# Second feed-forward output of a two-layer block: the sum for the second block product made one step earlier, four loads in another order, and a plan that starts with two engines taken

## The chip, the cores and the metric

The kernel runs on one core of a Trainium2 chip. Five engines work at the same time, each through its own instruction list in the order written: TensorE (PE in the profile, its weight loads PEld), VectorE (DVE), ScalarE (ACT), GpSimd (POOL) and SyncE (SP, which issues the loads). They wait for each other by semaphores. The metric is the device time of one execution in microseconds (us); the time before is the median of three runs.

## The reference

A block of depth 2 on 512 tokens with 1024 features: layer 0 has a gated recurrent mixer, layer 1 a dilated attention, and each is followed by a feed-forward part. All is float32. Only the feed-forward part of layer 1 matters here:

```python
D_MODEL, SEQ, D_FF = 1024, 512, 2816

def swiglu_ffn(u, w_in, w_out):
    gate, up = jnp.split(u @ w_in, 2, axis=-1)
    return (jax.nn.silu(gate) * up) @ w_out

# in reference(), for each layer, with mod = cond @ ada_w[layer] + ada_b[layer]
# split into sh1, sc1, g1, sh2, sc2, g2
        u = rms_norm(h, norm_g[layer, 2]) * (1.0 + sc2) + sh2
        y = swiglu_ffn(u, ffn_w_in[layer], ffn_w_out[layer])
        h = h + (1.0 + g2) * rms_norm(y, norm_g[layer, 3])
```

## The kernel before

**Float32 by parts.** Every operand of a matmul is split into a high part (a cast on ACT) and a low part (operand minus high part, on DVE). A product of two operands is three matmuls: high by high, high by low, low by high. So each new operand costs one ACT and one DVE instruction before TensorE can use it.

**The last step before the output.** The products into the 2816 hidden features run in `seven_products`, a loop over blocks of 128 features with seven block products in place of eight (the Strassen–Winograd form). The hidden features land in `midt`, the names of whose rows are `mid`. In the last pass of that loop an `OutStart` object is called (`sooner()`); it makes the first operands of the output stage: a high and a low part of a quarter of `mid`, the high and low parts of quarter 0 of the first weights in `uh` and `ul`, and the difference of weight quarters 1 and 0. The loop keeps short sums in `W`, a view of the tile `shared`, in eight places of 256 columns, half of them for even and half for odd passes.

**The output stage.** `out_planned` computes `mid` by the second weights: 11 blocks of 256 hidden features. The first four blocks (SEVEN = 4) are taken together as a matrix of two by two quarters and again multiplied with seven products: F, E, a second F, U, Z, a second E and a second U (the names are those of the PSUM banks that they add into; two banks each). Their four pairs of features are called a11, a12, a21, a22, the weight quarters 0 to 3. The other blocks, from block 4 on, are plain products with all four names. On TensorE the order is: F, E, block 4 into F and Z, second F, block 5 into F and Z, U, Z, block 4 into E, second E, second U, block 5 into E, blocks 4 and 5 into U, then blocks 6 to 10. Each of the seven products has four steps j = 0 to 3 of six matmuls. A step needs the cut operand of `mid` (`a_cut`: `hiq`, `loq`, a ring of two) and the cut quarter of the weights of its step (`b_cut`: `uh`, `ul`, a ring of four). A plain block needs its weights cut by halves (`plain_splits`, from `rawx`) and two rows of `mid` cut into `uh` and `ul` places.

Before the change the operand of product E is the sum a21 + a22 (`first_sum`), that of U this sum minus a11 (`second_sum`), that of the second U is a11 − a21 (`third_sum`), and the second E's is a12 minus the operand of U (`fourth_sum`). Weight quarters are overwritten with differences while the products run (`b_sub`).

**What sets the order.** `out_planned` does not issue instructions but adds tasks to a `Plan`, each with its engine, an assumed cost, what it reads and writes. The plan gives every task a due time, worked back from an ideal TensorE order, and runs a list scheduling with several rules; the trial in which TensorE ends first sets the order of every engine, SP's loads too. The plan assumes that all engines are free at its start. The instructions of the loop before (`seven_products`) are in a hand-written order. `ada` items are a conditioning vector's weights, accumulated on DVE (four instructions a load) into `shared`, then summed over partitions by an all-reduce on POOL, for the gate of the last update.

**Loads.** `items` lists all weight loads in order; the SP queue issues them in that order. Two places (`raw`) hold them throughout; the output stage opens four more (`rawx`), whose memory is that of tiles which `seven_products` reads until its last matmuls with `th`, `tl` and `spare`. Quarters 0 and 1 go to the two `raw` places. The list `turn` in `planner` says which place is used next; `done_with_raw` frees one and adds a load.

Of the kernel before, what the change touches and what calls it, by code (L numbers as in the profile page):

```python
# [11 lines left out]
F32 = mybir.dt.float32  # L12
# [305 lines left out]
def block_kernel(tc, x, c, positions, ada_w, ada_b, norm_g, hgrn_w_in, lower, hgrn_norm_g, hgrn_w_out,  # L318
# [8 lines left out]
    with ExitStack() as ctx:  # L327
# [249 lines left out]
        items += f1a + quarter_items() + f1b[SEVEN:SEVEN + 2] + last_gate[0] + f1b[SEVEN + 2:SEVEN + 3] + last_gate[1] + last_gate[2]  # L577
# [321 lines left out]
        def seven_products(fs, mid, seeded, spare, th, tl, sooner=None):  # L899
# [86 lines left out]
            with tc.manual_schedule(engines=ORDERED):  # L986
# [10 lines left out]
                for i in range(len(fs)):  # L997
# [42 lines left out]
        class OutStart:  # L1040
# [8 lines left out]
            def __call__(self):  # L1049
                self.ring = st.part_tiles(0)  # L1050
                (hi, lo), src = self.a_place(0), groups_of(self.midt, 0, 0, 0)
                act.copy(PLACED2(hi), SEEN2(src))
                dve.tensor_sub(PLACED2(lo), SEEN2(src), PLACED2(hi).bitcast(F32))
                for k in range(4):
                    raw = st.raw[st.done][:, k * 512:k * 512 + 512]
                    act.copy(uh[:, k], raw)
                    dve.tensor_sub(ul[:, k], raw, uh[:, k].bitcast(F32))
                for k in range(4):
                    one, two = (st.raw[st.done + q][:, k * 512:k * 512 + 512] for q in range(2))
                    dve.tensor_sub(one, two, one)  # L1060

        def out_planned(midt, begun, roll, parts):
# [3 lines left out]
            plan, ticks, at_item, ready_first, _, mm_of, slot, PE, ACT, DVE, POOL, COPY, done_with_raw, next_weights, split_place, products, condition = planner(extra, len(items), SEVEN)  # L1066
            raws = [next_weights() for _ in range(SEVEN)]
# [82 lines left out]
            def plain_splits(j):  # L1150
                raw, p = next_weights(), split_place(0)
# [54 lines left out]
            product(E, first_sum, 0, True, lambda j, b: b_sub(j, 0, 3, 0))  # L1206
# [8 lines left out]
            done_with_raw(2)  # L1215
# [6 lines left out]
            product(U, third_sum, 1, False)  # L1222
# [476 lines left out]
        def planner(extra=(), end=0, held=0):  # L1699
# [1053 lines left out]
```

## Time and profile before

| what | value |
|---|---|
| runs (median; lowest to highest) | 1438.81 us; 1438.64 to 1441.27 us, 3 runs |
| profiled execution | 1441.98 us, span 1440.2 us |
| TensorE busy | 1406.5 us, 98% of the span |
| VectorE, ScalarE, GpSimd busy | 1152.0 (80%), 823.0 (57%), 209.8 us (15%) |
| granted TensorE clock, mean | 0.995 |
| output stage, first matmul to the span's end | 1315.4 to 1440.2 us |

The times of the trace are microseconds from the start of the span. A row of the timeline has the start, the duration, the engine, the line, the operation with what it writes and reads, how often, and in brackets the idle time of its engine before it and what ended that. Successive instructions of one engine can overlap by a few hundredths or tenths of a microsecond, so the distance from start to start is the price in a full queue, not the duration. Row of a wait: the engine, the line, what it waited for, the time in total, how often, the longest. The line numbers are those of the code above; in the changed kernel the same lines stand up to 27 further down.

### The profile page before, as it was taken

The page shows a single profiled execution, that of the slowest core. Times are in us where ns is not written, and L with a number is a line of the kernel's source. Part 1 is how long each engine was busy: PE and PEld are TensorE (multiplying, and loading weights), DVE is VectorE, ACT ScalarE, POOL GpSimd, SP SyncE. Part 2 cuts the span into 40 slices and gives each one's busy share as a digit, 9 for nine tenths or more (in the row PEclk, how much of TensorE's full clock was granted, in tenths as well). Part 3 has the DMA queues.
Part 4 walks back from the last instruction along what each step waited for, and adds up shares of the span by engine and source line. Part 5 has one row for each costly group of instructions (what it writes and reads, how often), then busy time and mean ns, then how long its engine had stood idle before and what let it go on. Part 6 is the DMA issues. An engine that isn't in the chain of part 4 may idle for free. (4 is left out here: it accounts for less than half of the span.)

```text
span 1440.2 us, 25201 instructions
## 1 busy us (share of the span) xinstructions
PE 1406.5 (98%) x9785; PEld 1303.5 (91%) x9785; DVE 1152.0 (80%) x1836; ACT 823.0 (57%) x1538; POOL 209.8 (15%) x179
## 2 busy tenths in 40 slices
PE   8999999999999999999999999999999999999998
PEld 6788899899999988888998989999988999998887
DVE  4499889587888799687887877888776978887984
ACT  4443434465555543376647878478886555555651
POOL 1013112130111112140001010001012211110030
PEclk9999999999999999999999999999999999999999
DMA  9565655132344377423253452444351334444341
GB/s 309 163 217 191 205 176 176 59 111 77 108 117 118 118 267 270 142 104 128 66 164 111 126 137 66 122 138 136 104 204 66 117 90 118 118 118 166 127 176 59
DMA packets 213896, 201.09 MB, mean 140 GB/s; under 512 B 8920, under 2 KB 170640, under 8 KB 213520
## 3 DMA queue, kind: packets, MB, share of 16 engines
q1 hardware_dynamic: 210800, 192.71, 42.8%
q10 hardware_dynamic: 1952, 6.65, 1.2%
q8 instruction: 77, 1.26, 0.4%
q0 software_dynamic: 1024, 0.12, 0.2%
q14 instruction: 43, 0.35, 0.1%
HBM read 192.30 MB, written 5.30 MB: 137 GB/s over the span
## 5 line engine op out<-in xcount | busy, mean ns | idle before, releaser
L1836 PE MATMUL ps_mm<-apart,hiq 128*128 128x256 f32 (+1 forms) x608 | 138.3, 322 | 2.1 <-ACT xs L2328 1.2
L1836 PE MATMUL ps_mm<-uh,hiq 128*128 128x256 f32 (+1 forms) x416 | 134.8, 324 | 2.8 <-ACT ps_mm L2303 2.8
L1836 PE MATMUL ps_mm<-uh,loq 128*128 128x256 f32 (+1 forms) x416 | 131.4, 316 | 0.2 <-DVE loq L2261 0.2
L1836 PE MATMUL ps_mm<-ul,hiq 128*128 128x256 f32 (+1 forms) x416 | 131.3, 316 | 0.0
L1836 PEld LDWEIGHTS ps_mm<-apart,hiq 128*128 128x128 f32 x608 | 100.8, 193 | 8.1 <-ACT xs L2328 1.7
L966 DVE TENSOR_TENSOR loq<-raw,hiq 128x1024 fp32r<-128x1024 f32 x72 | 85.0, 1221 | 20.1 <-ACT hiq L962 20.1
L975 PE MATMUL ps_mm<-th,hiq 128*128 128x256 f32 x360 | 99.0, 275 | 0.0
L975 PE MATMUL ps_mm<-tl,hiq 128*128 128x256 f32 x360 | 99.0, 275 | 0.0
L975 PE MATMUL ps_mm<-th,loq 128*128 128x256 f32 x360 | 99.0, 275 | 0.0
L1836 PE MATMUL ps_mm<-apart,loq 128*128 128x256 f32 (+1 forms) x304 | 95.8, 315 | 0.6 <-DVE loq L2350 0.6
L946 POOL TENSOR_TENSOR raw<-raw 128x512 f32<-128x512 f32 x36 | 47.9, 1331 | 319.9 <-DVE spare L942 165.2
L1836 PEld LDWEIGHTS ps_mm<-uh,hiq 128*128 128x128 f32 x416 | 79.5, 191 | 7.5 <-ACT ps_mm L2303 3.2
L962 ACT CAST hiq<-raw 128x1024 fp32r<-128x1024 f32 x72 | 72.1, 1047 | 21.1 <-DVE raw L950 16.5
L1836 PEld LDWEIGHTS ps_mm<-uh,loq 128*128 128x128 f32 x416 | 79.7, 192 | 4.7 <-DVE loq L2261 0.4
L1836 PEld LDWEIGHTS ps_mm<-ul,hiq 128*128 128x128 f32 x416 | 79.6, 191 | 4.1 <-issue 0.5
L975 PEld LDWEIGHTS ps_mm<-tl,hiq 128*128 128x128 f32 x360 | 69.1, 192 | 0.0
L975 PEld LDWEIGHTS ps_mm<-th,hiq 128*128 128x128 f32 x360 | 69.1, 192 | 0.0
L975 PEld LDWEIGHTS ps_mm<-th,loq 128*128 128x128 f32 x360 | 69.1, 192 | 0.0
L1836 PEld LDWEIGHTS ps_mm<-apart,loq 128*128 128x128 f32 x304 | 58.5, 193 | 3.9 <-DVE loq L2350 1.0
L595 PE MATMUL ps_mm<-ul,hi 128*128 128x256 f32 (+1 forms) x176 | 55.3, 314 | 1.6 <-DVE ul L694 1.6
L594 PE MATMUL ps_mm<-uh,hi 128*128 128x256 f32 (+1 forms) x176 | 55.4, 315 | 0.0
L596 PE MATMUL ps_mm<-uh,lo 128*128 128x256 f32 (+1 forms) x176 | 55.2, 314 | 0.0
(545 smaller groups left out, 4841.0 us busy)
## 6 DMA issues: line engine op xcount, KB each, us to landing
raw<-in_ffn_w_in_dram SPq DMA_DIRECT2D x144, 256.0 KB, 3.9
raw<-in_ada_w_dram SPq DMA_DIRECT2D x30, 1024.0 KB, 5.9
raw<-in_attn_w_in_dram SPq DMA_DIRECT2D x64, 256.0 KB, 4.6
raw<-in_ffn_w_out_dram SPq DMA_DIRECT2D x13, 1024.0 KB, 6.1
raw<-in_attn_w_in_dram SPq DMA_DIRECT2D x12, 1024.0 KB, 5.2
raw<-in_hgrn_w_in_dram SPq DMA_DIRECT2D x11, 1024.0 KB, 5.3
rawx<-in_ffn_w_out_dram SPq DMA_DIRECT2D x9, 1024.0 KB, 5.0
third<-in_ada_w_dram SPq DMA_DIRECT2D x8, 1024.0 KB, 7.0
```

Source lines behind the costliest of these rows:

```text
L594: pe.matmul(ps, ah, bh, start=start, stop=False, skip_group_check=part)
L595: pe.matmul(ps, ah, bl, start=False, stop=False, skip_group_check=part)
L596: pe.matmul(ps, al, bh, start=False, stop=stop, skip_group_check=part)
L946: pool.tensor_add(r[:, 2], r[:, 2], r[:, 0])
L962: act.copy(hi, src)
L966: dve.tensor_sub(lo, src, hi.bitcast(F32))
L975: pe.matmul(LAID(ps), w[x][:, a], TAKE(us[kt][y]), start=begin and kt + m == 0, stop=kt == 3 and m == 2, skip_group_check=True)
L1836: pe.matmul(LAID(dst()), x, TAKE(y), start=begin and i == 0, stop=i == len(todo) - 1, skip_group_check=True)
```

## The change

- `OutStart` now also makes the operand of product E, by halves of two features: `sum_half` adds a21 and a22 into two free places of `W` (those of the other parity), `hi_half` and `lo_half` cut it into the ring's second place. The first half is made in `__call__`, between the other operands there; the high part of the second half and its low part in `further`, which is called after the two copies of the pass. The differences of the weight quarters move into `further` too.
- `first_sum` and `third_sum` go. `second_sum` makes a21 = a11 − a21 in place and then s1 = a22 − a21, which is the same operand of U as before; the second U takes a21 as it stands. The products and their order are the same.
- The loads of the six items behind the first layer's weights are reordered: quarters 0 and 1, block 4, quarter 2, block 5, quarter 3. `turn` starts with places 2 and 4, where blocks 4 and 5 now are.
- The plan begins with two tasks without an instruction: VectorE taken for 2.6 us and ScalarE for 1.6 us.

```diff
-        items += f1a + quarter_items() + f1b[SEVEN:SEVEN + 2] + last_gate[0] + f1b[SEVEN + 2:SEVEN + 3] + last_gate[1] + last_gate[2]
+        quarters = quarter_items()
+        items += f1a + quarters[:2] + f1b[SEVEN:SEVEN + 1] + quarters[2:3] + f1b[SEVEN + 1:SEVEN + 2] + quarters[3:] + last_gate[0] + f1b[SEVEN + 2:SEVEN + 3] + last_gate[1] + last_gate[2]
...
                     if sooner and not more:
-                        sooner()
+                        sooner(W[:, 5 - i % 2:8:2])
                     run(s.first, R, 1024, B21, False)
                     act.copy(W[:, 4 + i % 2], s.both)
                     act.copy(s.u4, s.u2)
+                    if sooner and not more:
+                        sooner.further()
                     run(s.u4, Sm, 512, t1, False)
...
-            def __call__(self):
-                self.ring = st.part_tiles(0)
+            def sum_half(self, n):
+                two = slice(2 * n, 2 * n + 2)
+                dve.tensor_add(self.spare, groups_of(self.midt, 1, 0, 0)[:, two], groups_of(self.midt, 1, 1, 0)[:, two])
+
+            def hi_half(self, n):
+                act.copy(PLACED2(self.a_place(1)[0][:, 2 * n:2 * n + 2]), SEEN2(self.spare))
+
+            def lo_half(self, n):
+                hi, lo = (t[:, 2 * n:2 * n + 2] for t in self.a_place(1))
+                dve.tensor_sub(PLACED2(lo), SEEN2(self.spare), PLACED2(hi).bitcast(F32))
+
+            def __call__(self, spare):
+                self.ring, self.spare = st.part_tiles(0), spare
                 (hi, lo), src = self.a_place(0), groups_of(self.midt, 0, 0, 0)
+                self.sum_half(0)
                 act.copy(PLACED2(hi), SEEN2(src))
                 dve.tensor_sub(PLACED2(lo), SEEN2(src), PLACED2(hi).bitcast(F32))
+                self.hi_half(0)
                 for k in range(4):
                     raw = st.raw[st.done][:, k * 512:k * 512 + 512]
                     act.copy(uh[:, k], raw)
                     dve.tensor_sub(ul[:, k], raw, uh[:, k].bitcast(F32))
+                    if k == 0:
+                        self.lo_half(0)
+                        self.sum_half(1)
+
+            def further(self):
+                self.hi_half(1)
                 for k in range(4):
                     one, two = (st.raw[st.done + q][:, k * 512:k * 512 + 512] for q in range(2))
                     dve.tensor_sub(one, two, one)
+                self.lo_half(1)
...
-            raws = [next_weights() for _ in range(SEVEN)]
+            first = [next_weights() for _ in range(SEVEN + 2)]
+            raws = [first[k] for k in (0, 1, 3, 5)]
+            plain_raw = {SEVEN: first[2], SEVEN + 1: first[4]}
+            plan.add("DVE", 2.6, None, goal=-9.0)
+            plan.add("ACT", 1.6, None, goal=-9.0)
...
-            def first_sum(g):
-                a_op(g, dve.tensor_add, s1, a21, a22)
+            def second_sum(g):
+                a_op(g, dve.tensor_sub, a21, a11, a21)
+                a_op(g, dve.tensor_sub, s1, a22, a21)
                 return a_cut(0, 0, g, *s1)
-
-            def second_sum(g):
-                a_op(g, dve.tensor_sub, s1, s1, a11)
-                return a_cut(0, 0, g, *s1)
-
-            def third_sum(g):
-                a_op(g, dve.tensor_sub, a21, a11, a21)
-                return a_cut(1, 0, g)
...
-            product(E, first_sum, 0, True, lambda j, b: b_sub(j, 0, 3, 0))
+            product(E, lambda g: a_cut(1, 0, g, ready=True), 0, True, lambda j, b: b_sub(j, 0, 3, 0))
...
-            product(U, third_sum, 1, False)
+            product(U, lambda g: a_cut(1, 0, g), 1, False)
```

What this does to the engines' lists is seen at three places. The first is VectorE at the border of the two stages. In the rows, `mid_11738` is `mid`, `raw_13603` holds quarter 0, `hiq_13764` and `loq_13765` are the ring of cut `mid` operands; `ul<-raw` are low parts of weight quarters, `ul<-mid` low parts for blocks 4 and 5. Before:

```order
L984 SCALAR_TENSOR_TENSOR mid_11738<-shared 128x512
L1053 TENSOR_TENSOR loq_13765<-mid_11738,hiq_13764 128x1024
L1057 TENSOR_TENSOR ul<-raw_13603,uh 128x512 x4
L1060 TENSOR_TENSOR raw_13603<-raw_13707,raw_13603 128x512 x4
L982 TENSOR_TENSOR shared<-shared,ps_b_11891 128x256
L983 TENSOR_TENSOR shared<-shared,ps_mm_11807 128x256
L984 SCALAR_TENSOR_TENSOR mid_11738<-shared 128x512
L1122 TENSOR_TENSOR shared<-mid_11738 128x1024
L1161 TENSOR_TENSOR ul<-mid_11738,uh 128x512 x2
L1116 TENSOR_TENSOR loq_13765<-shared,hiq_13764 128x1024
L1102 TENSOR_TENSOR ul<-raw_13603,uh 128x512 x2
```

With the change:

```order
L1054 TENSOR_TENSOR shared<-mid_11738 128x2x256
L1068 TENSOR_TENSOR loq_13765<-mid_11738,hiq_13764 128x1024
L1073 TENSOR_TENSOR ul<-raw_13603,uh 128x512
L1061 TENSOR_TENSOR loq_13765<-shared,hiq_13764 128x512
L1054 TENSOR_TENSOR shared<-mid_11738 128x2x256
L1073 TENSOR_TENSOR ul<-raw_13603,uh 128x512 x3
L1082 TENSOR_TENSOR raw_13603<-raw_13707,raw_13603 128x512 x4
L1061 TENSOR_TENSOR loq_13765<-shared,hiq_13764 128x512
L983 TENSOR_TENSOR shared<-shared,ps_b_11891 128x256
L984 TENSOR_TENSOR shared<-shared,ps_mm_11807 128x256
L1188 TENSOR_TENSOR ul<-mid_11738,uh 128x512
L1129 TENSOR_TENSOR ul<-raw_13603,uh 128x512
```

The whole sum (L1122) and the low part of the sum (L1116) have gone from the place ahead of E's first low part; as halves they stand four to ten rows further up. On ScalarE, from the same border to the cast of block 4's weights, the list was this (`hiq` from `rawx` is block 4, `uh<-raw` after the two copies are E's casts):

```order
L1016 COPY ps_mm_11857<-ps_mm_11807 128x256
L1026 COPY shared<-ps_mm_11857 128x256
L1027 ACTIVATE shared<-ps_b_11889 128x256
L1160 CAST uh<-mid_11738 128x512 x2
L979 ACTIVATE shared<-ps_mm_11857 128x256
L1115 CAST hiq_13764<-shared 128x1024
L1101 CAST uh<-raw_13603 128x512
L1160 CAST uh<-mid_11738 128x512 x2
L1101 CAST uh<-raw_13603 128x512 x2
L1154 CAST hiq_13858<-rawx_13844 128x1024
L1101 CAST uh<-raw_13603 128x512
```

With the change:

```order
L1017 COPY ps_mm_11857<-ps_mm_11807 128x256
L1057 CAST hiq_13764<-shared 128x512
L1029 COPY shared<-ps_mm_11857 128x256
L1030 ACTIVATE shared<-ps_b_11889 128x256
L1187 CAST uh<-mid_11738 128x512
L1128 CAST uh<-raw_13603 128x512
L1187 CAST uh<-mid_11738 128x512 x2
L980 ACTIVATE shared<-ps_mm_11857 128x256
L1128 CAST uh<-raw_13603 128x512
L1187 CAST uh<-mid_11738 128x512
L1128 CAST uh<-raw_13603 128x512
L1181 CAST hiq_13861<-rawx_13848 128x1024
```

E's first cast now follows one cast of `mid`; its fourth still stands behind block 4's. The third place is SyncE, the loads of this stage. Before, `rawx_13842` and `rawx_13843` are quarters 2 and 3, the next two blocks 4 and 5:

```order
L87 DMA raw_13603<-in_ffn_w_out_dram 128x4x512
L87 DMA raw_13707<-in_ffn_w_out_dram 128x4x512
L87 DMA rawx_13842<-in_ffn_w_out_dram 128x4x512
L87 DMA rawx_13843<-in_ffn_w_out_dram 128x4x512
L87 DMA rawx_13844<-in_ffn_w_out_dram 128x2x1024
L87 DMA rawx_13845<-in_ffn_w_out_dram 128x2x1024
```

With the change:

```order
L87 DMA raw_13603<-in_ffn_w_out_dram 128x4x512
L87 DMA raw_13707<-in_ffn_w_out_dram 128x4x512
L87 DMA rawx_13848<-in_ffn_w_out_dram 128x2x1024
L87 DMA rawx_13849<-in_ffn_w_out_dram 128x4x512
L87 DMA rawx_13850<-in_ffn_w_out_dram 128x2x1024
L87 DMA rawx_13851<-in_ffn_w_out_dram 128x4x512
```

Block 4 is now the first of the four loads into the new places, quarter 2 the second, block 5 the third, quarter 3 the last. Beside these places, five of F's matmuls (its second step) have moved behind 24 matmuls of the last step before, and further on the accumulations of the conditioning vector and the low parts have changed places on VectorE; one accumulation more stands ahead of the additions into U.

More of the change, by code (lines that the diff above doesn't have):

```diff
@@ L1696, in block_kernel, with planner @@
         pre.close()
[L1699 removed]
+        def planner(extra=(), end=0, turn=()):
             plan = Plan()
@@ L1725, in planner @@
             queue, seq, to_load, queue_order = [], [0], [st.loaded], []
-            turn = list(range(held, 2 + len(extra)))
+            turn = list(turn) or list(range(2 + len(extra)))
             def load_next(spot=None):
```

6 lines of the change are left out of this document (3 added, 3 removed).

## The prediction

> **What bounds the kernel now.** I read the engine totals first, then the waits of TensorE in the last stage, then that place in the timeline.
>
> ```profile
> PE 1406.5 (98%) x9785; PEld 1303.5 (91%) x9785; DVE 1152.0 (80%) x1836; ACT 823.0 (57%) x1538; POOL 209.8 (15%) x179
> ```
>
> TensorE is busy for 98% of the span. The change leaves every matmul in place, so all it can win is idle time of TensorE. The waits of TensorE from 1300 us to the end (total, times, longest), and the busy times of PE, PEld, DVE, ACT and POOL in a stretch behind them:
>
> ```profile
> PE ps_mm L1134 <- ACT uh L1101: 2.4, 2, 1.4
> PE ps_mm L1134 <- DVE ul L1102: 1.8, 2, 0.9
> ...
> 1336.00:1434.00 98.00, 98.00 (x455) 85.55 (x453) 78.16 (x104) 44.87 (x65) 13.96 (x5) 1.00 0.35 123
> ```
>
> There are four waits, all in product E, and from 1336 to 1434 TensorE has no gap at all. The timeline of product E, TensorE with the ACT and DVE work that it waits for:
>
> ```profile
> 1323.61 1.23 DVE L1122 TENSOR_TENSOR shared<-mid 128x1024 f32<-128x1024 f32 x1
> ...
> 1324.87 0.38 PE L1134 MATMUL ps_a<-uh,loq 128*128 128x512 f32 x1
> 1324.92 1.20 ACT L1115 CAST hiq<-shared 128x1024 fp32r<-128x1024 f32 x1 [2.08 <-DVE shared L1122]
> 1326.00 0.64 ACT L1101 CAST uh<-raw 128x512 fp32r<-128x512 f32 x1
> 1326.16 1.25 DVE L1116 TENSOR_TENSOR loq<-shared,hiq 128x1024 fp32r<-128x1024 f32 x1
> ...
> 1326.69 0.48 PE L1134 MATMUL ps_mm<-uh,hiq 128*128 128x512 f32 x1 [1.44 <-ACT uh L1101]
> 1327.33 0.68 DVE L1102 TENSOR_TENSOR ul<-raw,uh 128x512 fp32r<-128x512 f32 x1
> ...
> 1328.07 0.48 PE L1134 MATMUL ps_mm<-ul,hiq 128*128 128x512 f32 x1 [0.89 <-DVE ul L1102]
> ...
> 1331.36 1.04 ACT L1154 CAST hiq<-rawx 128x1024 fp32r<-128x1024 f32 x1 [2.49 <-DMA rawx<-in_ffn_w_out_dram]
> ...
> 1332.31 0.61 ACT L1101 CAST uh<-raw 128x512 fp32r<-128x512 f32 x1
> 1332.43 1.23 DVE L1155 TENSOR_TENSOR loq<-rawx,hiq 128x1024 fp32r<-128x1024 f32 x1 [0.88 <-ACT hiq L1154]
> ...
> 1332.97 0.48 PE L1134 MATMUL ps_mm<-uh,hiq 128*128 128x512 f32 x1 [0.97 <-ACT uh L1101]
> 1333.58 0.69 DVE L1102 TENSOR_TENSOR ul<-raw,uh 128x512 fp32r<-128x512 f32 x1
> ...
> 1334.32 0.48 PE L1134 MATMUL ps_mm<-ul,hiq 128*128 128x512 f32 x1 [0.86 <-DVE ul L1102]
> 1334.64 0.38 PE L1134 MATMUL ps_mm<-uh,loq 128*128 128x512 f32 x1
> ...
> 1335.50 0.38 PE L594 MATMUL ps_a<-hiq,uh 128*128 128x512 f32 x1
> ```
>
> Matmuls without a wait start 0.215 apart (1334.64 to 1335.50 are four steps). The last one of F starts at 1324.87; E has 24, so block 4 should start 25 steps later, at 1330.25. It starts at 1335.50. **The ceiling of the gain is 5.25 us.** Two chains make it. First, the sum a21+a22 starts at 1323.61, its high part ends at 1326.12, and the first cast of E's other operand stands behind it on ACT, the first low part behind the low part of the sum on DVE: 1326.69 − 1325.09 = 1.60, and at the second matmul 1.38 − 0.22 = 1.16. Second, E's fourth cast stands on ACT behind the cast of block 4, which waits for its load until 1331.36. The rest of the 5.25 is this (about 2.4) and 0.1 behind each start.
>
> **The sum a21+a22 moves into the last step before.** Its two halves on DVE, two high casts on ACT, two low parts on DVE now stand among these rows:
>
> ```profile
> 1311.87 1.38 ACT L1052 CAST hiq<-mid 128x1024 fp32r<-128x1024 f32 x1
> 1313.14 2.18 ACT L1056 CAST uh<-raw 128x512 fp32r<-128x512 f32 x4
> 1313.28 1.34 DVE L1053 TENSOR_TENSOR loq<-mid,hiq 128x1024 fp32r<-128x1024 f32 x1 [1.92 <-ACT hiq L1052]
> 1314.54 2.48 DVE L1057 TENSOR_TENSOR ul<-raw,uh 128x512 fp32r<-128x512 f32 x4
> ...
> 1316.94 2.48 DVE L1060 TENSOR_TENSOR raw<-raw,raw 128x512 f32<-128x512 f32 x4
> ...
> 1320.01 0.42 DVE L982 TENSOR_TENSOR shared<-shared,ps_b 128x256 f32<-128x256 f32 x1 [0.58 <-ACT shared L1026]
> ...
> 1321.22 1.34 ACT L1160 CAST uh<-mid 128x512 fp32r<-128x512 f32 x2 [0.96 <-PE ps_mm L975]
> ...
> 1322.03 0.63 PE L1181 MATMUL ps_b<-uh 128*128 128x512 f32 x2
> ...
> 1324.75 1.35 DVE L1161 TENSOR_TENSOR ul<-mid,uh 128x512 fp32r<-128x512 f32 x2
> ```
>
> No row has these half sizes. They lie between a 128x512 operation (0.60 from start to start, 2.48 for four) and half the 1.23 to 1.35 of the whole, so 0.60 to 0.68; I take 0.63. The first sum fits into the 1.92 of idle time ahead of 1313.28 and is free. DVE then carries three more (two low parts, one sum), 1.9 us, and reaches the row of 1320.01 at about 1321.2. That row frees the bank that L1181 writes at 1322.03: 0.4 us to spare. On ACT the first high cast delays the four uh casts by 0.63. The first matmul of F (1315.42 now) needs the first of them, which then ends at 1314.4; the new order also runs 24 matmuls of the last step ahead of five of F's, so that F's second low part may be late (1317.0) at no cost. I take zero for all of this; the bounds are 0 and 1 us, where both spares are missed. A gain is excluded: nothing waits here now.
>
> **Product E.** Its first operand is ready, and its first uh cast is ahead of two uh<-mid casts instead of behind the sum. ACT can do it from 1321.9 (behind the first uh<-mid cast, which starts at 1321.2 before and after, when its place is free), DVE its low part by 1323.3; TensorE asks at 1325.1. The first chain's 2.87 us are gone. For the fourth step, walk DVE from 1322.0 in its new order with starts 0.70 apart for uh<-mid low parts, 0.60 for E's, 0.65 for the value row and 1.15 for block 4: the fourth low part ends near 1329.3. TensorE asks at 1329.2. I leave 0.1 to 0.2 us there.
>
> **The loads.** Before, all four wait for the place that the step ahead frees, and then run back to back (clock, DMA share, GB/s at the row's end):
>
> ```profile
> 1320.88 2.36 SPq L87 DMA_DIRECT2D rawx<-in_ffn_w_out_dram  x4
> ...
> 1322.90:1333.10 10.20, 6.89 (x30) 5.15 (x29) 8.86 (x11) 5.69 (x9) 0.00 (x0) 1.00 1.02 398
> ```
>
> A load of 1.05 MB at 398 GB/s takes 2.63 us. Block 4 is the third and is read from 1331.36, so the first is in place two loads sooner, at 1326.1. The order change moves five matmuls of F behind the last readers of that place, so the loads can start 1.08 earlier: 1325.0. ACT comes to block 4's cast at 1325.7. The second wait is gone. Quarter 2 arrives at 1327.6 and quarter 3, last, near 1332.9; DVE wants quarter 3 first near 1339, behind both sums for product U. The later arrival costs nothing, and would cost only if it were 6 us later still.
>
> **VectorE behind E decides what stays of the gain.** From 1340 on it has no gap. I compare its work from 1314.54 to the additions into U, which TensorE needs at 1376.94:
>
> ```profile
> 1314.54:1374.66 60.12, 55.95 (x278) 48.48 (x277) 55.94 (x78) 36.16 (x54) 0.00 (x0) 1.00 0.44 151
> ...
> 1374.66 1.30 DVE L1227 TENSOR_TENSOR ps_b<-ps_b,gate 128x512 f32<-128x512 f32 x2
> ...
> 1376.94 0.38 PE L594 MATMUL ps_b<-hiq,uh 128*128 128x512 f32 x1
> ```
>
> Here 55.94 of 60.12 us are work, 4.18 are waits. The new list between the same two rows differs by: minus one whole sum (1.15) and one whole low part (1.17), plus one half sum and two half low parts (1.9), plus one accumulation of the conditioning vector (0.67), which the new order puts ahead of the additions. Net +0.25, so 56.2 us. Of the waits I keep 0.6, nearly all where the low part of U's operand waits for ACT, whose cast can start only when the second of U's two sums, now next to each other, is made. DVE reaches the additions at 1314.54 + 56.8 = 1371.3, and the first ends at 1372.0. TensorE, without the 5.25, asks at 1371.7. It starts near 1372.1, with the small wait in E counted. **The gain is 1376.94 − 1372.1, about 4.8 us.** At Z the walk is as close: its first low part ends about 0.1 us after it is asked for, which lies inside the same 4.8. Behind the additions the next feeding of TensorE has about 1 us to spare, and the loads are issued some 4 us sooner, since each place is freed by the same DVE rows.
>
> **Sum.** The profiled execution takes 1441.98 (span 1440.2); 1441.98 − 4.8 = 1437.2. It lies 3.17 over the median of the three runs, 1438.81. Taking the same 4.8 from the median: **1434.0 us**.
>
> **Rivals.** (1) *VectorE stays the bound.* If the waits do not vanish because the new list makes others, DVE needs 56.2 + 4.18 and reaches the additions at 1374.9; TensorE starts at 1375.6, a gain of 1.3: 1437.5. For it: the walk leaves tenths at three places. Against: most old waits come from the sum and from the late load. (2) *Nothing comes of it:* the last step loses its two spares, and E finds other waits; 0 to 1 us, about 1438.3. (3) *Slower: the loads share the queue.* If four loads in flight shared the bandwidth, all would land near 1332.9. ACT would cast block 4 then and E's fourth operand behind it, DVE would end that low part near 1335.9, and block 4 on TensorE would start at 1337.0, 1.5 later than now: 1440.3. It decides once block 4 lands later than 1331.4. Against it: the third load is read at 1331.36 while the queue still moves data until 1333.1. (4) *Slower: GpSimd locks VectorE out.* The all-reduce follows the last accumulation of its vector, which the new order moves from 1387 to about 1375.8:
>
> ```profile
> 1387.94 8.13 POOL L1786 PARTITION_ALL_REDUCE shared<-shared  x1 [83.83 <-DVE shared L1783]
> ...
> 1389.15 1.21 DVE L1155 TENSOR_TENSOR loq<-rawx,hiq 128x1024 fp32r<-128x1024 f32 x1
> ...
> 1401.26 4.13 POOL L1786 PARTITION_ALL_REDUCE shared<-shared  x1 [5.18 <-DVE shared L1783]
> ...
> 1402.21 3.27 DVE L1155 TENSOR_TENSOR loq<-rawx,hiq 128x1024 fp32r<-128x1024 f32 x1
> ```
>
> Beside the second one a 1.21 us operation takes 3.27 and ends as the all-reduce does; beside the first, in its early part, none is longer. If only the last 3.2 us block (from 1380.9), they meet work wanted at 1387 or later: no cost. If all 8.13 block, block 6's first low part ends at 1384.9 where TensorE asks at 1377.5: 7.4 lost against 4.8 won, 1441.4. The Trainium skill (SBUF — State Buffer, "Who interferes with whom") has it that a VectorE instruction with two SBUF inputs contends with a GpSimd instruction that reads SBUF and that the loser waits for the whole of it. By that rule alone the result is this rival's 1441.4; the operation at 1389.15, at its usual length, speaks for the shorter block.
>
> **How the numbers follow.** Forecast (gain 4.2 to 5.25, so 1433.6 to 1434.6): 0.60. Rival 1 (gain 1 to 4.2): 0.23. Rival 2: 0.08. Rival 3: 0.05. Rival 4: 0.04. A change under 0.2%, 2.9 us, cannot be told from none by such a measurement; faster thus means under 1435.9. That is the forecast, half of rival 1 and some luck of the measurement: 0.74. Slower means above 1441.7: rival 4 with anything added, and rivals 2 and 3 with unlucky runs: 0.06. The rest is 0.20. The range runs from the ceiling with half a microsecond for the runs' spread, 1433.1, to rival 1's 1437.5.
>
> **What would show it.** Right: no wait of TensorE above 0.3 us between F and block 4, block 4 starting near 1330.4 if the stage begins when it does now, ACT no longer waiting for a load at block 4's cast, DVE almost without idle time from 1314 to 1371. Wrong: a wait at L1181 or between the last step's matmuls (spares missed), a wait of TensorE for a low part in Z or for the additions of more than 1 us (rival 1), block 4's cast waiting until 1332 (rival 3), or long VectorE operations under the first all-reduce with TensorE waiting at block 6 (rival 4).

## The result and the profile after

| | before | changed |
|---|---|---|
| median of 11 runs each, us | 1439.20 (1436.83 to 1441.98) | 1433.25 (1430.78 to 1437.02) |
| ratio, 95% interval | | 0.9960 (0.9949 to 0.9972) |
| profiled execution, span, us | 1441.98, 1440.2 | 1430.78, 1429.0 |
| F's first matmul, us from the span's start | 1315.42 | 1308.66 |
| stage: from there to the last matmul, us | 118.28 | 113.85 |
| last matmul to the span's end, us | 6.53 | 6.52 |

The kernel is faster, by 0.40% (0.28 to 0.51%): 5.8 us with an interval of 4.0 to 7.3, against a forecast of 4.8. The two profiled executions differ by 11.2 us, and here a reader must look at where: 6.76 us of that lies ahead of F's first matmul, where TensorE does the same work. Only 118.28 − 113.85 = **4.43 us lie in the changed stage**. The rest is the subject of the first two experiments; from here on times are compared by the stage.

The engine totals of the changed kernel:

```profile
PE 1402.2 (98%) x9785; PEld 1300.5 (91%) x9785; DVE 1151.8 (81%) x1838; ACT 823.5 (58%) x1539; POOL 208.5 (15%) x179
```

They hardly move, and TensorE's share is 98% as before. The gain is time in which it waited: from F's first matmul to the end of the last, its idle time falls from 4.17 us (118.66 less 114.49 busy) to 0.27 (114.23 less 113.96), which is 3.90 of the stage's 4.43. The waits of TensorE from 1290 us to the end (total, times, longest):

```profile
PE ps_mm L1161 <- DVE ul L1129: 0.3, 1, 0.3
```

Before there were four, of 4.2 us together; one is left.

The timeline of the changed kernel at product E. E's first matmul follows F's last at the usual 0.22; ACT makes block 4's cast (L1181) with no wait for its load; the only stall is at E's fourth step, where the low part (L1129) stands behind block 4's low part (L1182) on DVE. The first row is DVE's last idle time ahead of it, a wait for ACT:

```profile
1317.67 0.69 DVE L985 SCALAR_TENSOR_TENSOR mid<-shared 128x512 f32<-128x512 f32 x1 [0.22 <-ACT shared L980]
...
1318.11 0.38 PE L1161 MATMUL ps_a<-uh,loq 128*128 128x512 f32 x1
...
1318.33 0.38 PE L1161 MATMUL ps_mm<-uh,hiq 128*128 128x512 f32 x1
...
1319.24 1.15 ACT L1181 CAST hiq<-rawx 128x1024 fp32r<-128x1024 f32 x1
...
1320.19 0.72 ACT L1128 CAST uh<-raw 128x512 fp32r<-128x512 f32 x1
...
1320.98 1.21 DVE L1182 TENSOR_TENSOR loq<-rawx,hiq 128x1024 fp32r<-128x1024 f32 x1
...
1322.11 0.68 DVE L1129 TENSOR_TENSOR ul<-raw,uh 128x512 fp32r<-128x512 f32 x1
1322.21 0.38 PE L1161 MATMUL ps_mm<-uh,hiq 128*128 128x512 f32 x1
...
1322.85 0.48 PE L1161 MATMUL ps_mm<-ul,hiq 128*128 128x512 f32 x1 [0.25 <-DVE ul L1129]
...
1323.16 0.38 PE L1161 MATMUL ps_mm<-uh,loq 128*128 128x512 f32 x1
...
1324.03 0.38 PE L595 MATMUL ps_a<-hiq,uh 128*128 128x512 f32 x1
```

1322.85 − 1322.21 and 1323.16 − 1322.85 are 0.64 and 0.31 where 0.215 is free of waits: 0.52 us lost. Block 4 starts 1324.03 − 1308.66 = 15.37 us behind F's start; before it was 20.08. The second stall has no wait row, since the matmul ahead of it is on record for 0.38 us and the gap from start to start is 0.39; the distances of starts show it. It is Z's first step, whose low part stands behind the last sum (L1149):

```profile
1343.27 1.22 DVE L1149 TENSOR_TENSOR mid<-mid,shared 128x1024 f32<-128x1024 f32 x1
...
1344.40 1.28 DVE L1129 TENSOR_TENSOR ul<-raw,uh 128x512 fp32r<-128x512 f32 x2
...
1344.75 0.38 PE L1161 MATMUL ps_mm<-uh,hiq 128*128 128x512 f32 x1
...
1345.14 0.48 PE L1161 MATMUL ps_mm<-ul,hiq 128*128 128x512 f32 x1
...
1345.46 0.38 PE L1161 MATMUL ps_mm<-uh,loq 128*128 128x512 f32 x1
```

0.39 + 0.32 − 0.43 = 0.28 lost. 5.25 − 0.52 − 0.28 = 4.45: the two stalls account for what the stage's 4.43 us leave of the ceiling. VectorE from E's preparation to the additions into U (busy PE, PEld, DVE, ACT, POOL):

```profile
1307.78:1364.84 57.06, 56.79 (x284) 49.70 (x283) 56.14 (x80) 38.54 (x57) 0.00 (x0) 1.00 0.48 166
```

and in the timeline the additions and TensorE's first matmul behind them:

```profile
1364.84 1.29 DVE L1247 TENSOR_TENSOR ps_b<-ps_b,gate 128x512 f32<-128x512 f32 x2
...
1365.75 0.38 PE L595 MATMUL ps_b<-hiq,uh 128*128 128x512 f32 x1
```

VectorE has 56.14 us of work in 57.06, where before it was 55.94 in 60.12: 0.92 us of idle time are left in the whole stretch. TensorE comes to the additions without a gap.

### The profile page after: what moved, and what is told of

Its sections match the earlier page's. It is cut to its first block, busy times and chain, and to the rows that moved or that the text cites. A ratio compares the mean times of both kernels' runs of the same rounds, so it can differ in the third digit from the quotient of the medians.

```text
span 1429.0 us, 25206 instructions
## 1 busy us (share of the span) xinstructions
PE 1402.2 (98%) x9785; PEld 1300.5 (91%) x9785; DVE 1151.8 (81%) x1838; ACT 823.5 (58%) x1539; POOL 208.5 (15%) x179
```

## The experiments

The stage runs from F's first matmul to the last matmul, read from each kernel's timeline; the clock is read from windows.

| kernel | F starts at | half clock in the stage | stage, us |
|---|---|---|---|
| before; before_again | 1315.42; 1311.70 | 0; 3.4 | 118.28; 118.39 |
| changed; after_again | 1308.66; 1309.08 | 0; 0 | 113.85; 113.93 |
| sums_only; sums_only_2 | 1312.51; 1309.59 | 6.8; 6.8 | 119.93; 119.83 |
| loads_only; loads_only_2 | 1314.20; 1313.85 | 3.4; 3.4 | 117.37; 117.61 |
| no_plan_lines | 1314.73 | 0 | 115.51 |
| one_more_sum | 1310.79 | 0 | 115.04 |
| two_more_sums | 1310.58 | 3.4 | 117.95 |
| early_fourth | 1311.61 | 0 | 113.77 |
| fourth_and_gpsimd | 1314.18 | 3.4 | 117.00 |
| low_parts_first | 1313.85 | 0 | 113.68 |

"Half clock" is the time behind a wait in this stage in which the granted clock stood at 0.50. (The last microseconds of every profile, with few matmuls left, have it too; they are left out here.)

### The two kernels once more

Expected of the kernel before, unchanged:

> The kernel before, a second profile. Both profiles taken so far count their stage from the first matmul of product F to the last matmul: 118.28 us before, 113.85 after; ahead of F the pair differs by another 6.76 us (F starts at 1315.42 and 1308.66). Theory (what lies ahead of the stage is chance from run to run, the stage is not): the stage comes out at 118.3 +- 0.15 again, F's start anywhere from 1308 to 1316. Rival (the change also moved something ahead of F): F starts within 0.5 of 1315.4 again. Against which the later profiles of the changed kernels are to be held.

Expected of the changed kernel, unchanged:

> The changed kernel, a second profile. Theory (the stage repeats, what lies ahead of it is chance): stage 113.85 +- 0.1, with the same two small losses (about 0.5 at E's fourth step, 0.3 at Z's first), F's start anywhere from 1308 to 1316. Rival (the changed kernel is also earlier at F): F's start at 1308.7 +- 1 again.

The stage repeats within 0.11 us: 118.28 and 118.39, 113.85 and 113.93, a gain of 4.43 and 4.46. F's start does not repeat: 1315.42 and 1311.70 before the change. Over all fourteen profiles it lies between 1308.66 and 1315.42. The seven that have the changed kernel's instructions ahead of F (it, its repeat, and the kernels with more sums or another order behind F) lie between 1308.66 and 1314.18, so most of the 6.76 us can be chance. Part of it is the clock: ahead of F the first profile of before has 10.2 us at a granted clock of 0.50 and that of the changed kernel 3.4, and with the same matmuls TensorE is busy for 1292.0 and 1288.2 us. Both profiles of the changed kernel (1308.66 and 1309.08) are at the low end, though, and two profiles can't exclude a small share that is not chance.

Not expected: the second profile of the kernel before has 3.4 us of half clock within product E, between its two waits, and yet its stage is the same. The load that E's fourth step waits for came when it came; TensorE, at half speed, only waited less for it (one gap of 0.89 us where the first profile has two of 1.35).

### Each half of the change alone

The early operand with the old load order:

```diff
 # the changed kernel, with the loads as before
-        items += f1a + quarters[:2] + f1b[SEVEN:SEVEN + 1] + quarters[2:3] + f1b[SEVEN + 1:SEVEN + 2] + quarters[3:] + last_gate[0]
+        items += f1a + quarter_items() + f1b[SEVEN:SEVEN + 2] + last_gate[0]
...
-planner(extra, len(items), (2, 4))
+planner(extra, len(items), (4, 5))
```

> The changed kernel with the old load order (block 4 third of the four loads behind F's start); the early operand of E and the two plan lines stay. Theory (two chains in series in E; the later one covers the earlier): E starts without a wait, but block 4's cast waits for the third load, 1.08 earlier than before because the loads are issued earlier: from 14.9 us behind F's start. E's fourth low part ends near 18.0, block 4 starts on TensorE near 18.8 behind F's start (20.08 before, 15.37 after), stage 117.0 us, a gain of 1.3. Rival (the sum's 2.87 is a gain of its own): block 4 at 17.2, stage 115.4.

The new load order with the old sums:

```diff
 # the kernel before, with the loads as in the change
-        items += f1a + quarter_items() + f1b[SEVEN:SEVEN + 2] + last_gate[0]
+        items += f1a + quarters[:2] + f1b[SEVEN:SEVEN + 1] + quarters[2:3] + f1b[SEVEN + 1:SEVEN + 2] + quarters[3:] + last_gate[0]
...
-            raws = [next_weights() for _ in range(SEVEN)]
+            first = [next_weights() for _ in range(SEVEN + 2)]
+            raws = [first[k] for k in (0, 1, 3, 5)]
```

> The kernel before with the new load order alone; E's operand is made behind F as before, no plan lines. Theory: the loads are issued 5.46 us behind F's start as before, block 4 is in place by 10.6, the second chain's 2.4 us go, the sum's 2.87 stay: block 4 starts 17.7 us behind F's start, stage 115.9 us, if VectorE follows (it had 1.6 us to spare at the additions into U). Rival (VectorE is the bound behind E, whatever the loads do): stage 117.0, with a wait of more than 0.8 us at the additions into U or in Z. Rival (the loads do nothing alone): 118.3.

Both came out longer than the theory: 119.93, which is 1.6 *slower* than before, and 117.37, a gain of 0.9 only. In both the clock had fallen to half behind the wait. Was that chance?

> The changed kernel with the old load order, a second profile: the first had 6.8 us of half clock behind its 3.2 us wait, and a stage of 119.93. Theory (the clock falls to half for multiples of 3.4 us when the wait fills enough of a stretch of 3.4 us, so that it depends on where the wait lies to that beat): the wait at E's fourth step is 3.2 +- 0.1 again; the half clock may last 0, 3.4 or 6.8 us, the stage is 117.2, 118.7 or 119.9. Rival (the half clock there came from something else): 117.2 with no half clock. Without the half clock's share 117.2 in each case: the gain of the early operand alone is 1.1.

> The kernel before with the new load order alone, a second profile: the first had 3.4 us of half clock behind E's two first waits, and a stage of 117.37. Theory as in the other repeat: stage 115.7 to 115.9 without half clock, 117.4 with 3.4 us of it. Rival: 117.4 with no half clock, so that the load order is worth only 0.9.

It came again, in the same length. The second profile of the early operand alone, ACT and TensorE at E's fourth step:

```profile
1322.93 0.38 PE L1158 MATMUL ps_mm<-uh,loq 128*128 128x512 f32 x1
1324.42 1.04 ACT L1178 CAST hiq<-rawx 128x1024 fp32r<-128x1024 f32 x1 [4.16 <-DMA rawx<-in_ffn_w_out_dram]
1325.38 0.61 ACT L1125 CAST uh<-raw 128x512 fp32r<-128x512 f32 x1
...
1326.04 0.79 PE L1158 MATMUL ps_mm<-uh,hiq 128*128 128x512 f32 x1 [2.74 <-ACT uh L1125]
```

and two windows behind it (busy PE, PEld, DVE, ACT, POOL, then the granted clock, DMA share and GB/s):

```profile
1326.00:1329.40 3.40, 2.81 (x6) 1.94 (x7) 2.77 (x4) 3.40 (x6) 0.00 (x0) 0.50 0.05 19
1329.40:1332.80 3.40, 3.40 (x10) 2.67 (x9) 3.40 (x6) 3.40 (x7) 0.00 (x0) 0.50 0.70 214
```

Block 4's cast waits for the third load until 14.83 us behind F's start (expected: 14.9), and E's fourth step behind it has a gap of 3.11. Then come two windows of 3.40 us at a clock of 0.50, in which matmuls start 0.43 apart instead of 0.215. Taking the extra distance of each matmul out (2.66 us) leaves 117.2, what the theory expected (117.0): the early operand alone is worth 1.1 us of waits, because E's stall then moves to the load. In the two profiles of the load order alone the extra distances come to 1.48 and 1.70 us, and the stage without them is 115.9 in both (expected: 115.9), a gain of 2.4.

So without the clock the parts give 1.1 and 2.4, together 3.5; with it they give −1.6 and +0.8. Both at once give 4.45. A half of this change, tried by itself, would have looked like a loss. The rivals have no support: the operand as a gain of its own would have given 115.4, and with the loads alone there is no wait in Z or at the additions into U, which VectorE as the bound would have shown.

**When the clock falls.** The same stretch, with E's first two waits (gaps of 1.82 and 1.38, nearly the same in each profile that makes the sum behind F), in the kernel before:

```profile
1324.70:1328.10 3.40, 1.06 (x5) 0.37 (x3) 3.25 (x5) 3.18 (x5) 0.00 (x0) 1.00 1.06 400
1328.10:1331.50 3.40, 3.40 (x16) 3.00 (x17) 3.12 (x4) 0.91 (x3) 0.00 (x0) 1.00 1.02 407
```

and in the second profile of the load order alone:

```profile
1323.40:1326.80 3.40, 1.06 (x4) 0.48 (x3) 3.00 (x4) 3.40 (x6) 0.00 (x0) 1.00 1.05 405
1326.80:1330.20 3.40, 3.40 (x11) 2.75 (x10) 3.38 (x5) 3.40 (x6) 0.00 (x0) 0.62 1.02 395
```

TensorE is busy for 1.06 of 3.40 us in both, and the clock stays in one and falls in the other. Of the four profiles with this pair of waits, three have 3.4 us of half clock behind it.

What differs is where the pair lies on a beat. In each profile all changes of the clock lie whole multiples of 3.413 us apart (in before_again at 775.55, 778.96, 1325.10 and 1328.51). Counted between the marks of this beat, the period with most of the pair has TensorE busy for 1.22, 1.48 and 1.59 us in the three profiles whose clock falls; in the fourth the marks divide the pair so that this period has 1.97. The other falls in the table come behind periods with 0.63 to 1.45 us, and the longest wait without a fall, 1.69 in one_more_sum, leaves 2.12. Busy time is not the whole rule: at the end of the stage, periods with 1.42 and 1.44 us did not bring the clock down.

The Trainium skill (TensorE: Matmul & The Clock Gate, "Part 1: The HAM clock gate") says that the gate watches a free-running window of about 3.4 us, so that the same kernel can come out differently. The lengths of 3.4 and 6.8 us, the beat, and the unequal outcome of equal waits fit that. The Trainium skill puts the fall there behind at least one idle window; here it came without any 3.4 us of idle time, behind single gaps of 2.4 to 3.2 us and behind that pair.

### The two lines that begin the plan

```diff
-            plan.add("DVE", 2.6, None, goal=-9.0)
-            plan.add("ACT", 1.6, None, goal=-9.0)
```

> The changed kernel without the two lines that begin the plan with VectorE and ScalarE taken. The planner then takes VectorE to be free when the last step still needs it, and sets the first sum for product U (128x1024, 1.26 us) into the last step, ahead of three of its own subtractions; E's first casts come behind all four casts of mid. Theory (the last step has 0.4 us to spare at the bank that its value row frees and E's first operand 2 us): the value row comes 1.2 later, TensorE waits in F or at E's start, 0.5 to 1.5 us: stage 114.4 to 115.4 us instead of 113.85. Rival (the lines only reorder work that has slack): 113.85 +- 0.2. Rival (the sum is better there, since it relieves VectorE later): 113.3.

Stage 115.51 us, 1.66 worse than with the lines, a little over the range of the theory. DVE and TensorE in that kernel; L1147 is the sum that now comes early, L1206 two matmuls of which the second needs the bank that DVE frees:

```profile
1317.69 0.69 DVE L1082 TENSOR_TENSOR raw<-raw,raw 128x512 f32<-128x512 f32 x1
...
1318.30 1.22 DVE L1147 TENSOR_TENSOR mid<-mid 128x1024 f32<-128x1024 f32 x1
...
1319.43 1.89 DVE L1082 TENSOR_TENSOR raw<-raw,raw 128x512 f32<-128x512 f32 x3
...
1321.34 0.40 PE L1206 MATMUL ps_b<-uh 128*128 128x512 f32 x1
...
1321.86 0.41 DVE L983 TENSOR_TENSOR shared<-shared,ps_b 128x256 f32<-128x256 f32 x1
...
1322.33 0.50 PE L1206 MATMUL ps_b<-uh 128*128 128x512 f32 x1 [0.59 <-DVE shared L983]
```

The same bank in the changed kernel:

```profile
1314.69 0.42 DVE L983 TENSOR_TENSOR shared<-shared,ps_b 128x256 f32<-128x256 f32 x1
...
1315.27 0.63 PE L1208 MATMUL ps_b<-uh 128*128 128x512 f32 x2
```

The DVE row ends at 1315.11. The first of the two matmuls does not need it (in the rows above it starts at 1321.34, before the DVE row there), and the second starts at 1315.51: 0.40 us to spare and no wait. Without the lines 0.85 us is lost at the bank and 1.62 in three waits for low parts in E, against 0.80 in all with them. So the lines carry more than a third of the gain: they keep the planner from putting 1.13 us of VectorE where only tenths are free.

### VectorE behind E: the amount

```diff
-                a_op(g, dve.tensor_sub, s1, a22, a21)
+                a_op(g, lambda *o: [dve.tensor_sub(*o) for _ in range(3)], s1, a22, a21)
```

> The changed kernel with the second sum for product U made three times instead of once (the result is the same; the planner knows nothing of it, so every order stays): 2.3 us more of VectorE between E and U (1.14 from start to start of each). Theory (VectorE has no time to spare behind E and decides what stays of the gain): Z's first low part, already 0.28 late, is 2.0 to 2.3 later, stage 115.9 to 116.2 us; up to 1.7 more if a half-clock period of 3.4 us falls behind the wait. Rival (VectorE has slack there, and the small wait in Z is the cast's or a load's): stage below 114.4.

> The changed kernel with the second sum for product U made twice instead of once (the result is the same, every order stays): 1.14 us more of VectorE. Made three times, it cost Z a wait of 2.7 us and 3.4 us of half clock behind it, stage 117.95. Theory (each 1.14 us of VectorE there is 1.14 us of wait in Z, whatever the clock does): the wait in Z is 1.3 to 1.5 us. What the clock does behind a wait of this size no run has shown: waits of 2.2 us and more in one piece halved it for 3.4 us or more, losses of 0.9 us and less did not. If it falls, the stage is 116.4 to 116.8 us; if not, 115.0 to 115.2. Rival (VectorE gives way elsewhere, since the planner's order leaves slack): stage below 114.6.

Z's first low part, its matmul in the kernel with one more sum:

```profile
1346.77 0.38 PE L1161 MATMUL ps_mm<-uh,hiq 128*128 128x512 f32 x1
...
1348.46 0.48 PE L1161 MATMUL ps_mm<-ul,hiq 128*128 128x512 f32 x1 [1.31 <-DVE ul L1129]
```

and with two more:

```profile
1346.74 0.38 PE L1161 MATMUL ps_mm<-uh,hiq 128*128 128x512 f32 x1
...
1349.64 0.79 PE L1161 MATMUL ps_mm<-ul,hiq 128*128 128x512 f32 x1 [2.52 <-DVE ul L1129]
...
1350.23 0.63 PE L1161 MATMUL ps_mm<-uh,loq 128*128 128x512 f32 x1
```

The gap grows from 0.39 to 1.69 and 2.90. One sum more, of 1.14 us on DVE, makes the stage 115.04, 1.11 to 1.19 longer: one to one. Two more make it 117.95; 1.52 of that are matmuls at half clock (the starts behind the wait are 0.42 to 0.43 apart for 3.4 us), and without them 116.4 remain, 2.5 to 2.6 over the changed kernel for 2.28 of added work. VectorE has no time to spare between E and Z. The half clock came behind the 2.90 gap and not behind the 1.69 one.

### VectorE behind E: the order

E's casts and low parts marked urgent, so that the fourth stands ahead of block 4's:

```diff
-                    ACT(0.52, lambda: act.copy(b.t[0], at(q, j)[0]), [key], [b("h")])
+                    ACT(0.52, lambda: act.copy(b.t[0], at(q, j)[0]), [key], [b("h")], urgent=soon)
# the low part (DVE) in the same way; product(E, ..., soon=True) for the first E
```

> The changed kernel with E's casts and low parts marked urgent for the planner: E's fourth low part comes ahead of block 4's on VectorE (and its cast ahead of block 4's). It takes away the 0.52 us that TensorE loses at E's fourth step. Theory (VectorE is the bound from E to Z; its work up to Z's first low part is the same): the 0.52 comes back as a longer wait in Z, 0.28 becomes 0.7 to 0.8, stage 113.85 +- 0.15. Rival (the two losses are separate): stage 113.3.

E's stall is gone, no gap from F to block 4, and Z's is back, larger:

```profile
1346.09 1.26 DVE L1149 TENSOR_TENSOR mid<-mid,shared 128x1024 f32<-128x1024 f32 x1
...
1347.19 0.38 PE L1161 MATMUL ps_mm<-uh,hiq 128*128 128x512 f32 x1
1347.23 0.72 DVE L1129 TENSOR_TENSOR ul<-raw,uh 128x512 fp32r<-128x512 f32 x1
...
1348.01 0.48 PE L1161 MATMUL ps_mm<-ul,hiq 128*128 128x512 f32 x1 [0.44 <-DVE ul L1129]
```

0.82 + 0.32 − 0.43 = 0.71 lost in Z instead of 0.52 + 0.28 at two places; stage 113.77. The theory holds and the rival (113.3) falls: what TensorE gains at E it waits for at Z. The row of the sum names the next suspect, and two kernels take it away from there. One gives it to GpSimd:

```diff
-                a_op(g, dve.tensor_sub, a12, a12, s1)
+                POOL(2.6, lambda: pool.tensor_sub(a12[0], a12[0], s1[0]), [a12[1], s1[1]], [a12[1]])
```

> As the run with E's urgent casts, and with the last sum (a12 less the second sum, 128x1024, 1.14 us of VectorE just ahead of Z's first low part) on GpSimd. Theory (VectorE's work ahead of Z is what is missing): both losses go, stage 113.05 +- 0.1, which is the 118.28 of before less the whole ceiling of 5.25. Rival (GpSimd's sum, some 2.5 us of two SBUF inputs, holds up VectorE's operations beside it for as long): stage 113.8 or more, VectorE operations of over 2 us beside it. Rival (Z waits for ScalarE or a load): 113.3 to 113.6.

The rival for GpSimd holds. Its sum and the DVE work beside it:

```profile
1338.57 1.89 DVE L1135 TENSOR_TENSOR raw<-rawx,raw 128x512 f32<-128x512 f32 x3
...
1338.82 5.26 POOL L1223 TENSOR_TENSOR mid<-mid,shared 128x1024 f32<-128x1024 f32 x1 [35.95 <-DVE shared L1149]
...
1340.38 1.52 DVE L1143 TENSOR_TENSOR loq<-shared,hiq 128x1024 fp32r<-128x1024 f32 x1
...
1341.82 3.41 DVE L1129 TENSOR_TENSOR ul<-raw,uh 128x512 fp32r<-128x512 f32 x2
```

The sum is on record for 5.26 us. DVE works at its usual pace through the first 3.0 of them; then two low parts take 3.41 instead of 1.28, 2.13 more, and Z's first step loses 2.25. With 1.69 of half clock behind that, the stage is 117.00. The work given away was 1.14.

The other leaves the sum on VectorE and lets Z's first two low parts go ahead of it:

```diff
-                a_op(g, dve.tensor_sub, a12, a12, s1)
+                DVE(cost(g, 1.15), lambda: dve.tensor_sub(a12[0], a12[0], s1[0]), [a12[1], s1[1], z_low[1]("l")], [a12[1]])
# z_low: the places of Z's low parts, in order; product(E) and product(Z) with soon=True
```

> The changed kernel with the casts and low parts of E and Z marked urgent, and the last sum (a12 less the second sum) held back, on VectorE as before, until Z's second low part is made. VectorE's total work is the same; only 1.14 us of it moves from ahead of Z's first low part to behind the fourth, with one 0.60 subtraction coming ahead instead. Theory (what is lost of the gain is the order on VectorE, not its amount: the additions into U have 0.9 us to spare in the run with E's urgent casts): E's 0.52 goes, Z's 0.71 shrinks to 0 to 0.2, stage 113.05 to 113.25 us; 1430.5 or a little more at the unchanged head, which a timing with an uncertainty of over 1 us cannot tell from the changed kernel. Rival (VectorE's amount is the bound): the loss comes back at the additions into U, stage 113.6 to 113.9. Rival (the late sum is itself late for the last product E): a wait there, stage over 113.9.

Here my theory fell. The stage is 113.68, within the rival's range. Z still loses 0.27 (one 0.60 subtraction now stands ahead of its low part), a low part of the second U 0.20, and the additions into U 0.17:

```profile
1369.91 1.29 DVE L1249 TENSOR_TENSOR ps_b<-ps_b,gate 128x512 f32<-128x512 f32 x2
...
1370.38 0.38 PE L597 MATMUL ps_mm<-hiq,ul 128*128 128x512 f32 x1
...
1370.66 0.48 PE L595 MATMUL ps_b<-hiq,uh 128*128 128x512 f32 x1
```

Three orders of the same VectorE work (changed, early_fourth, low_parts_first) lose 0.80, 0.71 and 0.64 of the ceiling, each at other places. In the last one VectorE itself is idle for 1.40 us between F's start and the additions, waiting for casts (54.66 us of work in 56.06), where the changed kernel has 0.92 (55.26 in 56.18): the new order makes new waits. Whether some order wins the whole 5.25 stays open. Timed against the kernel before, this one has a median of 1433.82 (10 runs) against 1438.55 (13 runs), a ratio of 0.9969 (0.9956 to 0.9982): faster than before, and not to be told from the changed kernel.

## Why the prediction was right

**The ceiling.** 5.25 us, worked out from distances of starts, is confirmed by the sum: 5.25 less the measured stalls of 0.80 is 4.45, and the stage moved by 4.43 and 4.46.

**The last step at no cost.** Right: E starts without a gap, F has none, L1208 no wait. The spare at the bank was put at 0.4 and is 0.40, but by two errors that cancel. DVE came to the row 6.03 us behind F's start, where the walk had 5.78, mainly since the three rows of half size cost 2.10 us from start to start and not 1.9; and the walk counted to the first of the two matmuls, where only the second needs the bank that this row frees. The bounds of 0 to 1 us were in place: the run without the plan lines, which sets 1.13 us there, lost 0.85 at the bank.

**E's operand and the loads.** Right. The four loads are issued 4.39 us behind F's start instead of 5.46, 1.07 earlier (1.08 forecast), and block 4's cast finds its data. Rival 3 (loads sharing the queue) has nothing for it: the cast reads block 4 at 1319.24, 6.19 us behind the issue at 1313.05, without a wait, and with the old load order (sums_only_2) the third of the four loads is read 10.45 us behind the issue, where it was 10.48 before.

**E's fourth step: the term that was too small.** Forecast 0.1 to 0.2, measured 0.52. The walk had the low part end 13.9 us behind F's start (the distances that it lists give 13.66) and TensorE asking at 13.8; it ended at 14.13. The step's cast was done 1.2 us before (1320.91 against 1322.11), so DVE was late. It began this list 0.11 later than in the walk. Its value row (L985) then waited 0.22 for ACT, where two casts of `mid` had come 0.75 apart instead of 0.60 to 0.63; with this wait the low part ahead of that row took 1.09 instead of 0.70, and two later ones 0.75. The repeat has the same: a wait of 0.27 there, and a gap of 0.70 at the fourth step instead of 0.64. And the start behind a wait costs 0.1 more, which the forecast counted for other waits and not for this one.

**Z.** Forecast 0.1, measured 0.28: 0.18 late and 0.1 behind the start. Together the two terms are 0.80 where some 0.25 were expected.

**VectorE and the additions into U.** The walk gave 56.8 us (56.2 of work, 0.6 of waits) and the trace has 57.06 (56.14 and 0.92). Its reading, that VectorE decides what is left of the gain, is what the experiments show: one more sum costs its own length. The place was only half right. It was to bind at the additions into U; in the changed kernel it binds at E's fourth step and Z, and TensorE reaches the additions late enough that they cost nothing. Forecast gain 4.8, measured 4.45 in the stage.

**The median.** It moved by 5.95, more than the ceiling of 5.25, with 1434.0 forecast and 1433.25 measured. 1.5 us of that are not in the stage. The stage's 4.45 lies within the interval of 4.0 to 7.3, and F's start varies by 6.8 between profiles. That 1433.25 is this near to 1434.0 is therefore partly luck: from the gain of the stage alone it would have been 1438.81 − 4.45 = 1434.4, or 1434.75 from the later median of before. Whether part of the 1.5 is a real difference ahead of F stays open.

**Rivals.** Rival 1 in its strong form (old waits come back elsewhere, gain 1.3) did not come: 0.92 us of VectorE's waits were left of 4.18. Rival 2 (0 to 1 us) fell with the stage's 4.43. Rival 4 (the all-reduce locks VectorE out for all of its 8.13 us) did not either. The all-reduce in the changed kernel, the last two DVE operations beside it, and the second all-reduce:

```profile
1369.34 7.35 POOL L1806 PARTITION_ALL_REDUCE shared<-shared  x1 [71.99 <-ACT uh L1187]
...
1372.77 0.84 DVE L1188 TENSOR_TENSOR ul<-mid,uh 128x512 fp32r<-128x512 f32 x1
...
1373.53 3.22 DVE L1182 TENSOR_TENSOR loq<-rawx,hiq 128x1024 fp32r<-128x1024 f32 x1
...
1388.68 3.23 POOL L1806 PARTITION_ALL_REDUCE shared<-shared  x1 [12.00 <-DVE shared L1803]
```

Operations are as long as ever until 1373.5, then one of 1.21 takes 3.22 and ends with the all-reduce, at a time when TensorE has work in store. The shorter block was the right reading.

## What to carry to other kernels

Two waits in a row on one engine are not two gains to be added: price each with the other still in place, and try both at once before giving up on either, since a half can lose where the whole wins. Where the engine behind a removed stall has no idle time, another order of its work mostly moves the remaining stall about, and each addition to that work costs its full length; count the work first. And compare profiles from the first instruction that the change touches, not by their spans.

## What was not expected of the hardware

- **The clock.** A wait of TensorE can cost more than itself. Behind gaps of 2.36, 2.90, 3.11 and 3.20 us, and in three of four profiles behind gaps of 1.82 and 1.38, the granted clock was 0.50 for 3.4 or 6.8 us, which cost up to 2.7 us more. Behind 1.69 and less it stayed. Whether that pair does it goes with where it lies on the beat of 3.413 us. The forecast had no term for it. It was right without one because in the kernel before the later wait for the load covers such a period, and in the changed kernel no wait is long enough.
- **GpSimd's length on record.** A GpSimd sum of 128x512 takes 1.28 us in this kernel's earlier stage; the one of 128x1024 beside a busy VectorE took 5.26, and held VectorE up only in its last 2.3. The all-reduce has the same form, 7.35 us with the last 3.2 blocking, where the second one has 3.23 in all. This reads as an instruction that first waits for VectorE and then shuts it out. The Trainium skill (SBUF — State Buffer, "Who interferes with whom") describes such an exclusive lock, taken by whoever issues first; a record that counts GpSimd's own wait would then explain both lengths. No run here separates the wait from the work, so this is argued, not shown.
- **ScalarE.** Casts of 128x512 from `mid` cost 0.68 to 0.83 us from start to start in the two profiles of the changed kernel and 0.60 to 0.63 in the first of before. Why stays open. The casts from `raw` and of block 4 look longer in one profile only (0.72 and 1.15 us on record, in the repeat 0.60 to 0.62 and 1.04, in before 0.61 to 0.64 and 1.04), but from start to start they cost 0.51 to 0.53 and 0.95 in all three, since the longer rows overlap the next.
